# The last store of a batched Q·Kᵀ kernel, cut into DMAs of 96, 25, 5 and 2 partitions

## The chip, the cores and the metric

One core of a Trainium2 chip. The metric is the device time of one execution in microseconds (us); lower is better.

## The reference

```python
batch, n_heads, seq, head_dim = 8, 12, 1024, 64     # q and k: float32
return np.einsum('bhid,bhjd->bhij', q, k).astype(np.float32)
```

96 heads, each with a 1024 x 1024 float32 result of 4 MB: 403 MB are written and 50 MB read.

## The kernel before

The inputs are cast to fp16 and transposed on the chip, ahead of the head that needs them; TensorE makes the scores, ScalarE copies them from PSUM to an SBUF tile `o_sb` of 128 partitions x 32 KB, and SyncE's queue stores that tile. The parts that matter here:

```python
def scores(self, n, side):
    ...
    o_sb = out_pool.tile([P, NT, S], F32, tag="out")      # 4 buffers of this tag
    for u in range(NT // 2):
        ...                                               # 4 matmuls, one copy on ScalarE
    pin(
        nc.sync.dma_start(
            out=of[self.first + n].rearrange("(p t) j -> p (t j)", p=P),
            in_=o_sb.rearrange("p t j -> p (t j)"),
        )
    )
```

Each partition's 32 KB go to a contiguous 32 KB of the output, so a store is 128 rows, and one row is one packet of a DMA engine: the trace of before has 12,288 packets of 32,768 bytes, 96 x 128.

## Time and profile before

| | before |
|---|---|
| time, median of 4 runs | 1068.37 us (1068.13 to 1069.23) |
| span in the profile | 1066.3 us |
| last store issued | 1033.64 us |
| completion increments of the last store | 1052.7 (first) to 1064.82 us (last) |
| of these, within 3.7 us of the first | 13 of 16 |
| one packet of 32 KB | 1.213 us |

Read it from the bottom. Each store has 16 completion increments, up to 12.1 us apart, and I read them as one from each of the 16 DMA engines of the page, with eight rows each (8 x 1.213 = 9.7 us, the time of a store in the steady state). The store is over with the last of the 16, at 1064.82 us here. The lines of the profile that carry this are in the prediction.

### The profile page before, as it was taken

Reading aid. Unit: us, or ns where it says so; the run is one execution under the profiler, and the core shown is the slowest. Engines: PE = TensorE matmul, PEld = TensorE weight load, DVE = VectorE, ACT = ScalarE, POOL = GpSimd, SP = SyncE. Lnnn points to the kernel's source line nnn. Section 1 sums busy time; section 2 is a strip of 40 time slices with the busy share of each in tenths; the row PEclk is TensorE's granted clock in tenths of the full one; section 3 lists DMA queues with packets and bytes.
Section 4 is the critical chain, followed back from the end, with each engine's and each line's share of the span. In section 5 each row is a group of like instructions: output and inputs, shape, how many; then the busy total and the mean of one; then the engine's idle time right before and its main releaser. Section 6 shows DMA issues by size and latency. Waiting matters only on the chain.

```text
span 1066.3 us, 4563 instructions
## 1 busy us (share of the span) xinstructions
PE 701.0 (66%) x1568; PEld 237.4 (22%) x1568; DVE 417.4 (39%) x101; ACT 694.5 (65%) x384; POOL 385.7 (36%) x382
## 2 busy tenths in 40 slices
PE   5997757576675766757666675666757667678750
PEld 2332222222221222222222221222212222222210
DVE  3856516236063360633606336063360632624000
ACT  2897666675766757667576666756667576777750
POOL 7794333433334333343334433344333443300000
DMA  9999999999999999999999999999999999999995
GB/s 386 418 433 428 434 431 431 429 435 427 434 429 434 426 434 428 437 423 437 428 433 427 435 427 432 429 434 427 435 426 436 426 434 437 430 433 431 432 433 247
DMA packets 28248, 453.29 MB, mean 425 GB/s; under 512 B 3136, under 2 KB 3136, under 8 KB 15936
## 3 DMA queue, kind: packets, MB, share of 16 engines
q1 hardware_dynamic: 15120, 406.33, 88.5%
q10 hardware_dynamic: 13104, 46.67, 10.8%
q8 instruction: 12, 0.20, 0.1%
q14 instruction: 12, 0.10, 0.0%
HBM read 50.33 MB, written 402.65 MB: 425 GB/s over the span
## 4 chain that ended last, share of the span: by engine, by line
DMA 76%; ACT 13%; PE 6%; DVE 1%; issue 0%; ACTq 0%; SPq 0%
DMA out_dram<-o_sb 72%; ACT o_sb L170 13%; PE ps L159 6%; DMA x_sb<-in_q_dram 3%; DMA early<-in_k_dram 1%; DVE o_sb L166 0%; DVE o_sb L168 0%; ACT o_sb L165 0%; PE ps L140 0%; ACT L165 0%; DVE kT L143 0%; ACTq L170 0%; ACTq L74 0%; SPq L174 0%
## 5 line engine op out<-in xcount | busy, mean ns | idle before, releaser
L159 PE MATMUL ps<-kT,qT 64*128 64x512 f16 x1536 | 697.2, 617 | 321.9 <-ACT o_sb L170 316.6
L170 ACT COPY o_sb<-ps 128x2048 f32<-128x2048 f32 x379 | 689.3, 1869 | 324.7 <-DMA out_dram<-o_sb 297.0
L115 POOL CAST half_sb<-x_sb 32x1024 f16<-32x1024 f32 x352 | 363.8, 1033 | 531.4 <-DMA x_sb<-in_k_dram 512.5
L132 DVE STREAM_TRANSPOSE qT<-half_sb 128x1024 f16<-128x1024 f16 x46 | 214.3, 4659 | 533.5 <-issue 533.5
L159 PEld LDWEIGHTS <-qT 64*128 64x128 f16 x1536 | 234.1, 157 | 783.1 <-issue 780.2
L132 DVE STREAM_TRANSPOSE kT<-half_sb 128x1024 f16<-128x1024 f16 x46 | 216.1, 4697 | 0.0
L115 POOL CAST half_sb<-early 32x1024 f16<-32x1024 f32 x16 | 16.5, 1033 | 2.4 <-DMA early<-in_k_dram 1.7
L140 PE MATMUL ps<-ident,half_sb 128*128 128x128 f16 x32 | 3.9, 309 | 8.8 <-POOL half_sb L93 6.1
L165 ACT ACT_TABLE_LOAD x1 | 1.3, 1283 | 11.4 <-DMA early<-in_k_dram 11.4
L166 DVE COPY o_sb<-ps 128x1024 f32<-128x1024 f32 x4 | 4.8, 1223 | 6.5 <-ACT o_sb L165 6.5
L93 POOL CAST half_sb<-early 128x512 f16<-128x512 f32 x8 | 4.7, 613 | 3.3 <-DMA early<-in_q_dram 3.2
L165 ACT COPY o_sb<-ps 128x1024 f32<-128x1024 f32 x4 | 4.0, 1014 | 3.0 <-PE ps L159 3.0
L143 DVE COPY qT<-ps 128x1024 f16<-128x1024 f16 x2 | 2.5, 1225 | 8.3 <-PE ps L140 8.3
L140 PEld LDWEIGHTS <-half_sb 128*128 128x128 f16 x32 | 3.3, 142 | 10.3 <-POOL half_sb L93 6.1
L143 DVE COPY kT<-ps 128x1024 f16<-128x1024 f16 x2 | 2.4, 1220 | 3.6 <-PE ps L140 3.6
L168 DVE COPY o_sb<-ps 128x2048 f32<-128x2048 f32 x1 | 2.3, 2292 | 2.0 <-PE ps L159 2.0
masks.py:199 POOL TENSOR_SCALAR_AFFINE_SELECT ident<-ident 128x128 f16<-128x128 f16 x1 | 0.3, 292 | 0.1
masks.py:197 POOL MEMSET ident<- 128x128 f16 x1 | 0.2, 204 | 0.3 <-POOLq L266 0.3
L266 POOL MEMSET const-float32-0.0<- 128x1 f32 x1 | 0.1, 98 | 0.2 <-issue 0.2
L266 POOL MEMSET const-bfloat16-1.0<- 128x1 bf16 x1 | 0.1, 101 | 0.0
L266 POOL MEMSET const-uint8-127<- 128x1 uint8 x1 | 0.1, 101 | 0.0
L266 POOL MEMSET const-float32-1.0<- 128x1 f32 x1 | 0.1, 98 | 0.0
## 6 DMA issues: line engine op xcount, KB each, us to landing
out_dram<-o_sb SPq DMA_DIRECT2D x96, 4096.0 KB, 36.6
x_sb<-in_k_dram ACTq DMA_DIRECT2D x44, 512.0 KB, 34.4
x_sb<-in_q_dram ACTq DMA_DIRECT2D x41, 512.0 KB, 34.3
x_sb<-in_q_dram SPq DMA_DIRECT2D x3, 512.0 KB, 10.2
early<-in_k_dram ACTq DMA_DIRECT2D x4, 256.0 KB, 5.0
early<-in_q_dram SPq DMA_DIRECT2D x4, 256.0 KB, 4.6
early<-in_q_dram SPq DMA_DIRECT2D x2, 512.0 KB, 7.2
early<-in_k_dram ACTq DMA_DIRECT2D x2, 512.0 KB, 7.3
```

Source lines behind the costliest of these rows:

```text
L93: nc.gpsimd.tensor_copy(out=self.halves[x][:, :, half], in_=self.raw[half][:, x].rearrange("p (r d) -> p r d", d=D),)
L115: nc.gpsimd.tensor_copy(out=dst[:, :, b], in_=raw[32 * b : 32 * b + 32, :, :, h],)
L132: pin(nc.vector.transpose(out=dst[:, two], in_=src[:, two]))
L140: pin(nc.tensor.transpose(t_ps[:, t], self.halves[x][:, t], ident))
L143: pin(nc.vector.tensor_copy(out=dst, in_=src))
L159: nc.tensor.matmul(ps[:, tt, js], qT[cs, g, 2 * u + tt], kT[cs, g, js])
L165: pin(nc.scalar.copy(out=dst[:, 0], in_=ps[:, 0]))
L166: pin(nc.vector.tensor_copy(out=dst[:, 1], in_=ps[:, 1]))
L168: pin(nc.vector.tensor_copy(out=dst, in_=ps))
L170: pin(nc.scalar.copy(out=dst, in_=ps))
L266: nc = _bacc.Bacc("TRN2", target_bir_lowering=False, num_devices=1)
```

## The change

The intent: at the end of the program three of the 16 DMA engines are behind, and the other thirteen have nothing left to do (a busy share of 0.19 of 16 from 1055.42 to 1059.05 us). The last store is cut so that some engines get more rows and others fewer: pieces of 96, 25, 5 and 2 partitions.

```diff
-            pin(
-                nc.sync.dma_start(
-                    out=of[self.first + n].rearrange("(p t) j -> p (t j)", p=P),
-                    in_=o_sb.rearrange("p t j -> p (t j)"),
-                )
-            )
+            dst = of[self.first + n].rearrange("(p t) j -> p (t j)", p=P)
+            src = o_sb.rearrange("p t j -> p (t j)")
+            cuts = [0, P]
+            if self.first + n == BH - 1:
+                cuts = [0, 96, 121, 126, P]
+            for lo, hi in zip(cuts, cuts[1:]):
+                pin(nc.sync.dma_start(out=dst[lo:hi], in_=src[lo:hi]))
```

## The prediction

> **What bounds the kernel now.** I read the page first, then the chain of waits, then the end of the run in ever finer windows. The page says that the DMA engines are full nearly to the end:
>
> ```profile
> span 1066.3 us, 4563 instructions
> ...
> DMA  9999999999999999999999999999999999999995
> ...
> HBM read 50.33 MB, written 402.65 MB: 425 GB/s over the span
> ...
> DMA 76%; ACT 13%; PE 6%; DVE 1%; issue 0%; ACTq 0%; SPq 0%
> DMA out_dram<-o_sb 72%; ACT o_sb L170 13%; PE ps L159 6%; DMA x_sb<-in_q_dram 3%; DMA early<-in_k_dram 1%; DVE o_sb L166 0%; DVE o_sb L168 0%; ACT o_sb L165 0%; PE ps L140 0%; ACT L165 0%; DVE kT L143 0%; ACTq L170 0%; ACTq L74 0%; SPq L174 0%
> ```
>
> The second line is the busy share of the 16 DMA engines by fortieths of the span: 9 everywhere, 5 in the last slice. 72% of the chain that ended last is stores, so nothing on the compute engines is worth time. The change touches one store of 96, so all that it can move lies in that last slice. Next, what the queue of SyncE waits for from 995 us on, and the compute of the last head:
>
> ```profile
> SPq L174 <- ACT o_sb L170: 37.5, 4, 9.4
> SPq L277 <- DMA out_dram<-o_sb: 30.8, 1, 30.8
> ```
>
> ```profile
> 1031.75 1.87 ACT L170 COPY o_sb<-ps 128x2048 f32<-128x2048 f32 x1
> 1033.64 0.33 SPq L174 DMA_DIRECT2D out_dram<-o_sb  x1
> ```
>
> The last store is issued at 1033.64 us, as soon as ScalarE's last copy is over, and the program then waits 30.8 us for it. A store of 4 MB occupies the engines for 9.7 us in the steady state, so most of the 30.8 us is queueing behind two older stores. The end itself, in windows of one packet (1.21 us); the last two numbers of each row are the busy share of 16 engines and GB/s:
>
> ```profile
> 1043.30:1053.00 9.70, 0.00 (x0) 0.00 (x0) 0.00 (x0) 0.00 (x0) 0.00 (x0) 1.00 0.98 422
> 1053.00:1054.21 1.21, 0.00 (x0) 0.00 (x0) 0.00 (x0) 0.00 (x0) 0.00 (x0) 1.00 0.57 244
> 1054.21:1055.42 1.21, 0.00 (x0) 0.00 (x0) 0.00 (x0) 0.00 (x0) 0.00 (x0) 1.00 0.32 135
> 1055.42:1056.63 1.21, 0.00 (x0) 0.00 (x0) 0.00 (x0) 0.00 (x0) 0.00 (x0) 1.00 0.19 81
> 1056.63:1057.84 1.21, 0.00 (x0) 0.00 (x0) 0.00 (x0) 0.00 (x0) 0.00 (x0) 1.00 0.19 81
> 1057.84:1059.05 1.21, 0.00 (x0) 0.00 (x0) 0.00 (x0) 0.00 (x0) 0.00 (x0) 1.00 0.19 81
> 1059.05:1060.26 1.21, 0.00 (x0) 0.00 (x0) 0.00 (x0) 0.00 (x0) 0.00 (x0) 1.00 0.13 54
> 1060.26:1061.47 1.21, 0.00 (x0) 0.00 (x0) 0.00 (x0) 0.00 (x0) 0.00 (x0) 1.00 0.06 27
> 1061.47:1062.68 1.21, 0.00 (x0) 0.00 (x0) 0.00 (x0) 0.00 (x0) 0.00 (x0) 1.00 0.06 27
> 1062.68:1063.89 1.21, 0.00 (x0) 0.00 (x0) 0.00 (x0) 0.00 (x0) 0.00 (x0) 1.00 0.06 27
> 1063.89:1066.00 2.11, 0.00 (x0) 0.00 (x0) 0.00 (x0) 0.00 (x0) 0.00 (x0) 1.00 0.00 0
> ```
>
> Multiply the share by 16: 0.19 is three engines, 0.13 two, 0.06 one. So from about 1055.4 us only three engines work, and for the last 3.6 us a single one. One engine alone moves 27 GB/s, which is 1/16 of the 432 GB/s of the full stage: an engine does not speed up when the others stop. The trace's packet records say the same: every packet of the last store is one partition's row of 32,768 bytes and takes 1.213 us, early and late, and each engine starts its next packet every 1.21 us.
>
> The trace also has the 16 completion increments of every store, one per DMA engine. For the last store they fall at 1052.7 (three of them), 1053.0, 1054.2 to 1056.4 (nine), 1060.0, 1061.4 and 1064.82 us. I call the distance to the first the lag: three engines lag by 7.3, 8.7 and 12.1 us, the other thirteen by 0 to 3.7. The lag is not of the last store: it grows through the run, from 0.7 us between first and last increment at the first store, to 2.7 near 124 us, 5.1 near 388, 8.0 near 654 and 10.7 near 886. After the last increment another 1.5 us passes to the end of the span (1066.3).
>
> [...]16 increments for each store, eight packets of 1.21 us per engine. No DMA here has a k below 16. [...]The trace shows three laggards but not their numbers.[...]
>
> **The change, part by part.** It removes one DMA of 128 partitions and adds four on the same queue.[...]
> - 96 partitions: k = 16, six each on all engines.
> - 25: k = 5, five each on engines 0 to 4.
> - 5: k = 5, one each on engines 0 to 4.
> - 2: k = 2, one each on engines 0 and 1.
>
> So engines 5 to 15 go from 8 packets to 6, a gain of 2 x 1.21 = 2.42 us each. Engines 0 and 1 go to 13, a cost of 5 x 1.21 = 6.05 us; engines 2 to 4 to 12, a cost of 4.84 us. The bytes are the same. The purpose is plain: take work off laggards and give it to engines that would stand idle. It works if the laggards are among 5 to 15.
>
> Then, with the lag of the old end as zero line: the slowest engine ends at 12.1 - 2.4 = 9.7 instead of 12.1. The other two laggards end at 6.3 and 4.9. An engine among 0 and 1 with a lag between 0 and 3.7 ends between 6.05 and 9.75; one among 2 to 4 at 8.5 at worst. The new end is therefore 9.7, a gain of 2.4 us. That the heaviest loaded engine would end just where the relieved laggard does (9.75 against 9.7) looks like a split that was chosen from measured lags, and this is half of my reason to believe that the laggards lie above 4. Had the maker known nothing, three laggards all out of the five low numbers have (11 x 10 x 9)/(16 x 15 x 14) = 0.29 of the cases.
>
> Costs: three more issues on SyncE's queue, 0.33 us each by the line above, about 1 us, from 1033.97 to 1035.0. The first engine reaches its part of the last store no sooner than about 1043.0, when the first increments of the store before fall (1043.03), so there are some 8 us of slack and nothing is lost. The extra DMAs take the next completion semaphores, last used by stores that landed at 996.7, 1006.5 and 1016.3, so none has to wait. A completion write takes 9 ns in the packet records; three more are nothing. No compute moves. Sum: -2.4 us.
>
> **Rivals.**
> - *A laggard is among engines 0 to 4.* The slowest there: its end moves to 12.1 + 4.8 or + 6.05, so the time rises by 4.8 to 6.05, to 1073.4 or 1074.6. Only the second (8.7) there: 13.5 or 14.75, so +1.4 to +2.65. Against it: the look of the split[...].
> - [...]the low engines would finish their six rows later, perhaps 1 to 3 us, before they turn to their seven more. An engine that ends at 6 to 9.75 without this would end at 8 to 13. That makes the time 1067 to 1071. [...]Against it: the laggards come so late that few engines would meet. I cannot rule it out; it is the main reason for a range that is longer upwards.
> - *k is 1 for 25 or 5 partitions*: one engine would get 30 rows more, 36 us, and the time would pass 1095.[...]
> - *The end is hidden anyway*: no. Nothing but the last increment releases the end.
>
> **Range and chances.** My best case, half of the weight, is 1068.5 - 2.4 = 1066.1; runs scatter by about half a microsecond (1068.21 to 1069.23). [...]the slowest engine among the loaded ones (one in seven) 1073 to 1075. I state 1066.3 with 1065.4 to 1072.0. Two per cent are 21 us, far more than anything here but the k = 1 case, so "within 2%" has 0.98; faster by 21 us is impossible while 403 MB must be stored.
>
> **What would show it.** Right: all lines of the page as before but the last; the store shown as four issues of 3072, 800, 160 and 64 KB; in the packet-wide windows no long stretch with a share of 0.06, and instead five to seven engines busy until about 1062; the last increment near 1062.4; packets still 1.21 us. Wrong: if the packets of the last store take longer than 1.21 us[...]; if one to five engines go on beyond 1065 with ordinary packets, a laggard was loaded; if one engine runs alone for tens of microseconds, k was 1.

k is the number of engines that a DMA runs on, and the numbers 0 to 15 are names. The sum of the forecast is -2.4 us, two packets of 1.21 us less on the slowest engine. The second rival: rows of the 96 that slow each other down. Its 1 to 3 us are a guess. It and a second laggard among the loaded engines had three chances in ten together, 1067 to 1071 us.

## The result

| | before | changed |
|---|---|---|
| time, median | 1068.37 us (1068.13 to 1069.23, 4 runs) | 1081.68 us (1076.49 to 1083.38, 4 runs) |
| span in the profile | 1066.3 us | 1074.7 us |
| last increment of the store before the last | 1055.15 us | 1061.53 us |
| last increment of all | 1064.82 us | 1073.73 us |

The ratio is 1.0124, with a 95% interval of 1.0086 to 1.0162; it counts a fifth run of the changed kernel, 1085.63 us, that the median leaves out. A ratio here is the mean time of one kernel's runs over that of the other's runs of the same rounds, so it is not quite the ratio of the medians. The change costs 13.3 us by the medians (1081.68 - 1068.37); this is far outside my range, which ended at 1072.0. The profiled execution of the changed kernel is the fastest of its runs (1076.49), so its trace shows the effect at its mildest.

The page of the changed kernel: of the DMA line only the last slice moved, from 5 to 3; stores are 69% of the chain, where they were 72%.

```profile
span 1074.7 us, 4566 instructions
...
DMA  9999999999999999999999999999999999999993
...
DMA out_dram<-o_sb 69%; ACT o_sb L170 13%; PE ps L159 6%; DMA x_sb<-in_q_dram 3%; DMA x_sb<-in_k_dram 3%; DMA early<-in_k_dram 1%; DVE o_sb L166 0%; DVE o_sb L168 0%; ACT o_sb L165 0%; PE ps L140 0%; ACT L165 0%; DVE kT L143 0%; ACTq L170 0%; SPq L181 0%; ACTq L74 0%
```

The list of DMA issues and the order of time of the changed kernel: the four pieces of the cut have the sizes I expected, and their issue starts at the same time as the single one did (1033.64) and is over by 1037.3, almost six us before a fast engine is free for them (1043.06). The four issues take 3.68 us in all, the three small ones 1.0 to 1.1 us each, where I had put 0.33.

```profile
out_dram<-o_sb SPq DMA_DIRECT2D x1, 3072.0 KB, 35.3
...
out_dram<-o_sb SPq DMA_DIRECT2D x1, 800.0 KB
out_dram<-o_sb SPq DMA_DIRECT2D x1, 160.0 KB
out_dram<-o_sb SPq DMA_DIRECT2D x1, 64.0 KB
```

```profile
1033.57 3.68 SPq L181 DMA_DIRECT2D out_dram<-o_sb  x4
```

Now the end of the changed kernel in windows; the last two numbers are the busy share of the 16 engines and GB/s, as in the rows of before in the prediction:

```profile
1033.60:1043.30 9.70, 0.00 (x0) 0.00 (x0) 0.00 (x0) 0.00 (x0) 0.00 (x0) 1.00 1.01 436
1043.30:1053.00 9.70, 0.00 (x0) 0.00 (x0) 0.00 (x0) 0.00 (x0) 0.00 (x0) 1.00 1.00 328
1053.00:1054.21 1.21, 0.00 (x0) 0.00 (x0) 0.00 (x0) 0.00 (x0) 0.00 (x0) 1.00 0.55 135
1054.21:1055.42 1.21, 0.00 (x0) 0.00 (x0) 0.00 (x0) 0.00 (x0) 0.00 (x0) 1.00 0.42 108
1055.42:1056.63 1.21, 0.00 (x0) 0.00 (x0) 0.00 (x0) 0.00 (x0) 0.00 (x0) 1.00 0.44 135
...
1068.00:1070.00 2.00, 0.00 (x0) 0.00 (x0) 0.00 (x0) 0.00 (x0) 0.00 (x0) 1.00 0.08 33
1070.00:1072.00 2.00, 0.00 (x0) 0.00 (x0) 0.00 (x0) 0.00 (x0) 0.00 (x0) 1.00 0.08 33
1072.00:1074.00 2.00, 0.00 (x0) 0.00 (x0) 0.00 (x0) 0.00 (x0) 0.00 (x0) 1.00 0.01 4
```

These rows teach the reading that decides the case. Divide GB/s by the number of busy engines (16 x share). Before, 0.57 and 244 give 26.8 GB/s for each busy engine, and 0.98 and 422 give 26.9. Changed, 1.00 and 328 give 20.5, and 0.55 and 135 give 15.3. The engines are busy and not moving their bytes: a packet takes longer. The packet records agree: from 1040 us on, all 198 packets of 32 KB of the kernel before took under 1.25 us, while of 199 in the changed kernel 55 took longer, up to 4.84 us, four times 1.213.

A second thing shows at the very end. The last increments of the four DMAs fall at 1068.84 (96 partitions), 1072.24 (25), 1073.73 (5) and 1064.66 us (2). The 5-partition DMA runs on engines 0 to 4, the 2-partition one on engines 0 and 1, and those two were through at 1064.66. So the program was ended by an engine among 2, 3 and 4, which still had extra rows to move.

So there were two suspects, and both had been my rivals: rows whose packets slow each other down when they move at the same time (theory P), and a laggard among the engines that got more rows (theory L).

### The profile page after: what moved, and what is told of

The parts are those of the page before. It is cut to its first block, busy times and chain, and to the rows that moved or that the text cites. A ratio compares the mean times of both kernels' runs of the same rounds, so it can differ in the third digit from the quotient of the medians.

```text
span 1074.7 us, 4566 instructions
## 1 busy us (share of the span) xinstructions
PE 700.9 (65%) x1568; PEld 237.2 (22%) x1568; DVE 417.4 (39%) x101; ACT 694.5 (65%) x384; POOL 385.6 (36%) x382
## 2 busy tenths in 40 slices
DMA packets 28260, 453.29 MB, mean 422 GB/s; under 512 B 3148, under 2 KB 3148, under 8 KB 15948
## 4 chain that ended last, share of the span: by engine, by line
DMA 76%; ACT 13%; PE 6%; DVE 1%; issue 0%; ACTq 0%; SPq 0%
DMA out_dram<-o_sb 69%; ACT o_sb L170 13%; PE ps L159 6%; DMA x_sb<-in_q_dram 3%; DMA x_sb<-in_k_dram 3%; DMA early<-in_k_dram 1%; DVE o_sb L166 0%; DVE o_sb L168 0%; ACT o_sb L165 0%; PE ps L140 0%; ACT L165 0%; DVE kT L143 0%; ACTq L170 0%; SPq L181 0%; ACTq L74 0%
```

## The experiments

### The rows alone, the load alone, and the number of DMAs

`pieces` lists (first row, last row, first column, last column) of each DMA of the last store; all other stores stay as they were. A row has 8192 columns of 4 bytes.

```diff
+            pieces = [(0, P, 0, NT * S)]
+            if self.first + n == BH - 1:
+                pieces = [(0, 96, 0, NT * S), (96, P, 0, NT * S)]              # cut96_32
+                pieces = [(0, P, 0, 6144), (0, 125, 6144, 8192),
+                          (125, P, 6144, 8192)]                               # load_only
+                pieces = [(0, P, 2048 * i, 2048 * i + 2048) for i in range(4)] # cols4
+            for lo, hi, c0, c1 in pieces:
+                pin(nc.sync.dma_start(out=dst[lo:hi, c0:c1], in_=src[lo:hi, c0:c1]))
```

**cut96_32.**

> The last store as two DMAs of 96 and 32 partitions, both on 16 engines: 6 and 2 packets each, so every engine still has 8 packets of 32 KB, as before; only which rows an engine takes differs from one DMA of 128. Theory P[...]: packets of 2 to 5 us show up at the end as in the changed kernel, and the time rises by 4 to 10 us over before (1068.4), to 1072 to 1079. Theory L (only the load moved to engines 0 to 4 costs, because a laggard is among them): no packet count differs from before, so within 1 us of before.

Measured: 1076.34 us (1074.46 to 1079.46), before 1068.48; ratio 1.0072 (1.0053 to 1.0092). Plus 7.9 us by the medians although every engine has eight packets of 32 KB by my count (96/16 + 32/16), as before. Its windows:

```profile
1043.30:1053.00 9.70, 0.00 (x0) 0.00 (x0) 0.00 (x0) 0.00 (x0) 0.00 (x0) 1.00 1.01 331
1053.00:1062.70 9.70, 0.00 (x0) 0.00 (x0) 0.00 (x0) 0.00 (x0) 0.00 (x0) 1.00 0.49 149
```

Full engines at 331 GB/s: 20.5 per engine, the same figure as in the changed kernel. What differs from before is only which rows an engine takes. This is theory P's number, and theory L has none for it. The delay lies in the store before the last: its last increment came at 1063.27 us, 8.1 later than in the kernel before (1055.15), and from there to the last increment of all it is 9.76 us (1073.03), where the kernel before has 9.67.

**load_only.**

> The last store as 128 partitions by 6144 columns (16 engines, the same rows per engine as before, 24 KB each) and the other 2048 columns as 125 partitions (5 engines, 25 rows of 8 KB each) and 3 partitions. Engines 0 to 4 get 12.3 rows' worth of bytes as in the changed kernel, the others 6[...]. Theory L (laggard among 0 to 4): the slowest of them carries 4.2 rows' worth more, 5 us, so 1071 to 1076. Theory P alone (laggards above 4): large part as fast as before, all laggards relieved by 2.4 us, the time falls to about 1066 to 1067[...].

Measured: 1074.13 us (1073.91 to 1075.03); ratio 1.0048 (1.0031 to 1.0065): plus 5.7 us. Its large part kept its pace: 119 of its 128 packets of 24 KB took 0.91 us, three quarters of 1.213 (the other nine up to 2.3), and the store before the last ended at 1055.25 us, as in the kernel before. In the windows

```profile
1043.30:1053.00 9.70, 0.00 (x0) 0.00 (x0) 0.00 (x0) 0.00 (x0) 0.00 (x0) 1.00 0.88 368
1053.00:1062.70 9.70, 0.00 (x0) 0.00 (x0) 0.00 (x0) 0.00 (x0) 0.00 (x0) 1.00 0.38 149
```

0.88 and 368 give 26.1 GB/s per busy engine. So a laggard among engines 0 to 4 costs its extra bytes: 4.25 rows' worth (12.25 less 8) x 1.21 = 5.1 us, and 5.7 were measured. Theory L holds as well. In the profiled execution the laggard was not engine 4 alone: the last increment, 1072.26 us, belongs to the DMA of 3 partitions, so one of engines 0 to 2 ended the program, while engines 3 and 4 had ended by 1070.67. The two parts together, 7.9 + 5.7 = 13.6 us, come close to the 13.3 for the change; as the runs of the changed kernel lie up to 7 us apart, so close an agreement is partly luck.

**cols4.**

> The last store as four DMAs of 128 partitions by 2048 columns: four DMAs as in the change, but the same rows on the same engines as before. If the number of DMAs, their issue or their completion costs anything, it is here. Both theories: within 0.7 us of before. A third theory (four DMAs by themselves cost the 8 to 13 us): 1076 and more.

Measured: 1068.68 us (1068.23 to 1069.23), ratio 0.9998 (0.9983 to 1.0013). Four DMAs instead of one cost nothing that can be seen. (Each is issued as soon as its columns are copied, from 1028.6 us on, in 0.33 us. The slower issues of the change are not tested by this run; in the changed kernel they were over before an engine was free.)

### Which engine lags

**probe5**, the first of two probe kernels.

```diff
+                pieces = [(0, P, 0, 7680), (0, 112, 7680, 8192), (112, 117, 7680, 8192),
+                          (117, 121, 7680, 8192), (121, 124, 7680, 8192),
+                          (124, 126, 7680, 8192), (126, 127, 7680, 8192),
+                          (127, 128, 7680, 8192)]
```

> The last store as 128 partitions by 7680 columns, then the last 512 columns in DMAs of 112, 5, 4, 3, 2, 1 and 1 partitions. [...]the completion increments of each tell at what time engines 0, 1, 2, 3, 4 had emptied their queues: the list of k engines has one time more than that of k - 1. Theory L: among the five times there is at least one 7 to 12 us after the first, on engine 2, 3 or 4. Theory P alone: all five within 4 us. The time stays within 1.5 us of before.

The time was 1068.18 us, so the probe disturbs nothing. The increments of the small DMAs, in us, as the trace has them. Each list also holds one early time, 0.4 to 1.3 us after the issue and left out here: in the changed kernel, too, the DMAs of 25, 5 and 2 rows show 6, 6 and 3 times, the first of each between 1035.2 and 1037.4 us, before a fast engine is free for the data at 1043.06. (The second DMA of one partition was issued only at 1055.6 us and tells nothing more.) The trace has no numbers of engines. I number them by these lists: engine 4 is the one that is in the list of five and not in that of four, engine 3 is in that of four and not in that of three, and so on. That the same number is the same engine in another run is assumed.

```
5 partitions: 1052.8  1053.4  1054.2  1054.7  1065.4
4 partitions: 1053.0  1053.6  1054.4  1054.9
3 partitions: 1053.1  1054.5  1055.1
2 partitions: 1053.3  1055.2
1 partition:  1053.5
```

Going down, from each list to the next, the others come about 0.2 us later and one is gone. In the changed kernel, likewise, the five times of the 25 rows come back 1.2 to 1.5 us later for the 5 rows, and two of those 1.2 and 1.8 us later for the 2 rows. The one at 1065.4 is gone with four partitions: it is engine 4's. Engine 4 is the slowest of all 16 (the last increment of the big part was at 1064.71), and engines 0 to 3 are within 2.0 us of each other. The prediction's premise that the slowest engine lies above 4 is false.

**probe_mid** asks about engines 3, 4 and 5 and two groups:

```diff
+                pieces = [(0, P, 0, 7680), (0, 110, 7680, 8192), (110, 116, 7680, 8192),
+                          (116, 121, 7680, 8192), (121, 125, 7680, 8192), (125, 128, 7680, 8192)]
```

> As probe5, with last DMAs of 110, 6, 5, 4 and 3 partitions (k = 11, 6, 5, 4, 3): tells engines 3, 4 and 5 singly, and 0-2, 6-10, 11-15 as groups. If engine 4 is always the slowest one, as in probe5, then the list of five has a time some 12 us after the first and the list of four has none. If the laggards wander from run to run, another engine or group shows it.

> probe5 once more. Fixed laggards: engine 4 again some 12 us behind and engines 0 to 3 within 4 us. Wandering laggards: another pattern among engines 0 to 4, while the slowest of all is again 12 us behind the first.

> probe_mid once more, to see whether the engines of the laggards stay the same: fixed laggards give engine 4 alone among 0 to 5 again, wandering ones do not.

Engine 4 was the slowest in all of the four runs: its small piece came at 1065.4, 1065.5, 1066.2 and 1066.1 us, and in each case the list of four partitions has no such time. The other laggards wander. In probe5, probe5_b and probe_mid engines 0 to 3 were within 2.5 us of each other; in probe_mid_b two of engines 0 to 2 came at 1064.8 and 1064.9 while the third came at 1055.5. So one laggard is the same in the four runs by these numbers, on two chips, and it is one of the five that the change loads; the second and third laggard are in other places from one execution to the next. The times were 1068.28 (probe5_b), 1068.86 (probe_mid) and 1068.77 us (probe_mid_b).

### What the rows do, by themselves

**micro_ports** only stores, with one DMA in flight: a tiny write on VectorE to the same tile waits for each.

```python
rows = [(0, 128), (0, 96), (32, 128), (0, 64), (0, 32), (0, 16), (0, 4),
        (96, 121), (121, 126), (126, 128), (0, 80), (0, 112)]
for i, (lo, hi) in enumerate(rows + rows):
    dst = of[i].rearrange("(p t) j -> p (t j)", p=P)
    nc.sync.dma_start(out=dst[lo:hi], in_=o_sb[lo:hi])
    nc.vector.memset(o_sb[:, 0:64], 0.0)
```

> A kernel that only stores (its output is wrong on purpose): one DMA in flight at a time, 32 KB rows, of partitions 0-127, 0-95, 32-127, 0-63, 0-31, 0-15, 0-3, 96-120, 121-125, 126-127, 0-79, 0-111, and all that once more. Theory P: 128 partitions take 8 packet times (9.7 us) with all packets at 1.21 us; [...]packets of about 2.4 us, so 0-63 take 9.7 us and 0-31 4.85 us as well as half the bandwidth; [...]0-95 take about 9.7 us although each engine has only 6 packets. [...]1.21 us for each packet, so 9.7, 7.3, 7.3, 4.8, 2.4, 1.2, 1.2 us.

The clauses ahead of rows 0-95 expected 4.85 us for rows 0-15 and for rows 0-3. The last sentence is for rows that do not slow each other down.

The output is wrong. In the order of time, the number in brackets is how long VectorE waited for the store ahead of it, in the order of the first seven of `rows`:

```profile
20.69 0.11 DVE L48 MEMSET o_sb<- 128x64 f32 x1 [11.30 <-DMA out_dram<-o_sb]
34.80 0.11 DVE L48 MEMSET o_sb<- 128x64 f32 x1 [14.00 <-DMA out_dram<-o_sb]
48.17 0.11 DVE L48 MEMSET o_sb<- 128x64 f32 x1 [13.26 <-DMA out_dram<-o_sb]
60.30 0.11 DVE L48 MEMSET o_sb<- 128x64 f32 x1 [12.02 <-DMA out_dram<-o_sb]
67.00 0.11 DVE L48 MEMSET o_sb<- 128x64 f32 x1 [6.59 <-DMA out_dram<-o_sb]
73.67 0.11 DVE L48 MEMSET o_sb<- 128x64 f32 x1 [6.55 <-DMA out_dram<-o_sb]
80.13 0.11 DVE L48 MEMSET o_sb<- 128x64 f32 x1 [6.36 <-DMA out_dram<-o_sb]
```

128 rows take 11.30 us, 96 of the same rows 14.00. And 4 rows take about as long as 32 (6.36 and 6.59). The packets, and the time from the first start to the last end; a row that nothing slows down takes 1.213 us in this trace. The engines are counted by the completion packets of each DMA (288 under 512 B in all, twice 144):

| rows | engines | packets (measured, median and longest) | from first to last (measured) |
|---|---|---|---|
| 0-95 | 16 | 1.24, 2.81 us | 12.64 us |
| 32-127 | 16 | 1.25, 2.83 | 11.95 |
| 0-111 | 16 | 1.23, 2.77 | 11.83 |
| 0-79 | 16 | 1.89, 2.70 | 11.78 |
| 0-63 | 16 | 2.55, 2.56 | 10.34 |
| 0-31 | 16 | 2.54, 2.57 | 5.23 |
| 0-15 | 16 | 4.86, 5.06 | 5.22 |
| 0-3 | 4 | 4.83, 4.90 | 5.13 |
| 96-120 | 5 | 1.21, 1.67 | 6.57 |
| 121-125 | 5 | 2.57, 3.80 | 3.84 |
| 126-127 | 2 | 2.52, 2.52 | 2.56 |

For 128 rows the packets took 9.89 us in all and each under 1.26: there no row slows another down. In the other shapes some do: the longest packets are 1.67 to 5.06 us. Rows 126 and 127 take 2.52 us each, twice 1.213, and rows 0 to 3 take 4.83, four times, as if they took turns. My written expectation of 9.7 us for 96 rows was too short by 2.9. One thing the runs leave open: in all of them partition p goes to the same place in its head's 4 MB of DRAM, so they show which rows slow each other down, but not whether they do so where they are read or where they are written. How a DMA deals its rows out to the engines is not shown either; an estimate of these times stood here, and it is cut because its assumption about where rows meet was not from these runs.

### Does any cut of the last store help?

Engine 4 ended last in the four probe runs, so only engines 0 to 3 may get more: k must be 4. A tail of 116 rows has that: both runs have 3152 packets under 512 B, 195 x 16 + 16 + 4 + 12 (four engines for the 116 rows). And the main part must have all 128 rows, whose packets were under 1.26 us in micro_ports.

```diff
+                pieces = [(0, P, 0, 6656), (0, 116, 6656, 8192), (116, P, 6656, 8192)]  # relief4
+                pieces = [(0, P, 0, 7168), (0, 116, 7168, 8192), (116, P, 7168, 8192)]  # relief4_small
```

> An attempt at a version that beats both. The last store as 128 partitions by 6656 columns (16 engines[...]), then columns 6656 to 8191 as 116 partitions (k = 4: engines 0 to 3, 29 rows of 6 KB each) and 12 partitions (k = 12). In rows of 32 KB: engine 4, the slowest in all four probe runs, gets 6.69 instead of 8, engines 0 to 3 get 12.1, the rest 6.5 to 6.7. If engine 4 alone sets the end and engines 0 to 3 lag by under 4 us: 1.6 us less, 1066.9. If one of engines 0 to 3 lags by 9 us or more, as in the second run of probe_mid: 9 + 5 = 14, so 2 us more, 1070.5.

> The same with 7168 columns on 16 engines and 1024 columns in the two tails: engine 4 gets 7.13 rows' worth (1.06 us less), engines 0 to 3 get 10.75 (3.3 us more). Engine 4 alone sets the end: 1067.4. A laggard of 9 to 10 us among 0 to 3: up to 1 us more, 1069.

relief4: 1066.03, 1072.53, 1069.42, 1074.57, 1066.81 and 1070.65 us in six runs, before 1067.87 to 1068.49; ratio 1.0023 (1.0005 to 1.0042). relief4_small: 1067.22 to 1072.90, ratio 1.0017 (1.0001 to 1.0033). The medians are 1070.03 and 1070.32, against 1068.30 for before. In the profiled execution, the 1066.03 one, the windows read

```profile
1053.00:1062.70 9.70, 0.00 (x0) 0.00 (x0) 0.00 (x0) 0.00 (x0) 0.00 (x0) 1.00 0.36 141
1062.70:1066.00 3.30, 0.00 (x0) 0.00 (x0) 0.00 (x0) 0.00 (x0) 0.00 (x0) 1.00 0.01 2
```

with the last increment at 1063.0 instead of 1064.82: relieving engine 4 does what the prediction hoped for in this execution. In other executions it is up to 6 us worse than before. That fits with the wandering laggards being among engines 0 to 3 in those, as the second run of probe_mid had it; but the slow executions have no trace, so this is argued and not shown. No cut that I tried is better than the kernel before.

### Where engine 4's lag comes from

Two kernels that only store, 96 times 4 MB from one constant tile, with the small DMAs of probe_mid at the end. The second also runs 1536 matmuls that depend on nothing:

```diff
+        for _ in range(16):                      # store_pe only, per store
+            nc.tensor.matmul(ps, w[:64, :P], w[:64])
```

> What makes engine 4 lag: 96 stores of 4 MB from one constant tile and the DMAs of probe_mid at the end, no loads, no compute (the output is wrong on purpose). If the lag is the engine's own slower pace: engine 4 is some 10 us behind at the end, and the spread of the last store's 16 increments is about 12 us. If it comes from other traffic of the program (instruction fetches, loads): spread under 3 us and engine 4 within it.

> store_only with 1536 matmuls of the kernel's shape that depend on nothing (output wrong on purpose): TensorE's instructions have to be fetched, about 200 KB as in the kernel. If the fetch of TensorE's instructions sits on engine 4 and costs it about 1 us for each of 12 fetches: engine 4 is 9 to 12 us behind at the end. If it is not the fetch: as store_only.

Both outputs are wrong. store_only (949.22 us): the 16 increments of the last big part fall within 1.2 us of each other (944.2 to 945.4), and engine 4 is not behind. In this run, then, engine 4 has no slower pace of its own. store_pe (951.15 us): within 3.0 us (944.3 to 947.3); the list of five has a time at 948.4, 2.3 us after the next, that the list of four does not have, so it is engine 4's. The list of DMA queues of store_pe has a row that store_only's does not have and that the kernel before has in the same size (packets, MB, share):

```profile
q8 instruction: 12, 0.20, 0.1%
```

So with TensorE's work engine 4 falls behind, but its lag behind the first increment is about 3 us (947.25 - 944.26), where the kernel before has 12.1. My expectation of 9 to 12 us was wrong, and that the 3 us come from the fetch of instructions is likely but not shown: it is one run, and the matmuls were added with their fetch.

The traces speak against the fetch as the rest. The 12 fetch packets of the kernel before took 0.88 to 1.06 us each. Near the one at 990.6 us the third largest lag jumps from 5.4 to 7.7 us, but the largest one does not: between 230 and 1024 us it grows from 2.8 to 12.1 in small steps, on average 0.13 us per store and once 0.7, also after the last load (914 us), and it stands still in the last three stores, after the last matmul (1031.7 us). In store_pe the largest lag is 4.3 us at the store that lands from 691.9 us on, soon after the last matmul (665.3), and falls to 3.0 by the end. What makes up the 12 us in the real kernel stays open.

## Why the prediction was wrong

- **What the change does to the packets** was right: four issues of the sizes named, k of 16, 5, 5 and 2 (28 completion packets), and no wait. The issues took 3.68 us and not the 1.3 of my sum, which the slack of 8 us hid.
- **"the laggards lie above 4"** is the step that failed first. The slowest engine is number 4 in four of four probe runs. I had taken the look of the split for a sign of measured lags. Neither was evidence about this kernel, and the trace of before could not tell the numbers. With the slowest engine among those loaded, the term of the sum is +4.84 us for four more rows, the value that I had written under the first rival; load_only, with 4.25 rows' worth more, measured +5.7.
- **The second rival**, rows that slow each other down, had the right effect and the wrong size: "perhaps 1 to 3 us" measured +7.9 (cut96_32). I had thought of the last store alone, where the isolated one with 96 rows is 2.75 us slower than the one with 128 (12.64 - 9.89). But at that time the laggards are still on the store before the last, and the engines that are ahead move rows of the 96 beside them. That this slows the older store shows in the traces: its last increment came at 1061.53 us in the changed kernel and at 1063.27 in cut96_32, against 1055.15 before and 1055.25 in load_only, where the large part has all 128 rows.
- **The rivals were taken one at a time.** They happen together. In the profiled execution they hit one engine, as the increments allow an estimate: counted back from 1072.24 us by eleven packets of 1.213 us, the engine that ended last left the store before the last no later than 1058.9, which fits the increment at 1058.39 and not the later two. That is 3.2 us after the last one of before; four more packets add 4.85, and 0.8 comes after, together the 8.9 between 1064.82 and 1073.73. The range should have had the sum of both in it.

Why the runs of the changed kernel scatter, 1076.49 to 1085.63 us, is not shown.

- **"within 2%" at 0.98** was right. Of the signs that I had named beforehand, two of the three for "wrong" came: packets over 1.21 us, and an engine going on beyond 1065 us.

## What to carry to other kernels

Before work is moved between DMA engines, measure which engine is behind, with a few small last DMAs of 5, 4, 3 partitions whose completion increments tell it, and do so in several executions, because only part of the pattern stayed the same here. Cut a transfer along its columns and leave all 128 partitions in it: cut along its partitions it can be slower with fewer bytes (cols4 1068.68 us against 1068.48 for before, cut96_32 1076.34; 96 rows alone 12.64 us, 128 rows 9.89). And when DMA engines are fully busy at fewer GB/s per engine than elsewhere in the same profile (328 at a share of 1.00 here, 436 at 1.01 in the window before), look for rows that slow each other down, and count the older transfers still under way among them.
